# GLU gate on one core: the last load and the last two stores split by rows, in place of eight column chunks of the last tile

## The chip, the cores and the metric

The kernel runs on one core of a Trainium2 chip. The time is that of one execution on the device, in microseconds (us); lower is better. A kernel is executed several times and the median is given with the lowest and the highest. All executions were fast, at a granted clock of 1.0.

The span on a profile page is a little shorter than the time of the same execution.

## The reference

```python
# x: 8192 x 8192, float32
def reference(x):
    a, b = np.split(x, 2, axis=-1)          # two halves of 4096 columns
    return a * (1 / (1 + np.exp(-b)))       # 8192 x 4096, float32
```

Every input element is read once and every output element written once: 268.44 MB in, 134.22 MB out, and a sigmoid and a multiplication per output element.

## The kernel before

A tile is 256 rows: 128 partitions with two consecutive rows each, so a partition's load is one contiguous piece of 64 KB and its store one of 32 KB. There are 32 tiles and two buffers each for input and output. SyncE issues the loads; ScalarE computes the sigmoid and also issues the stores; VectorE multiplies.

```python
x_t = x.rearrange("(n p r) m -> n p (r m)", p=P, r=PAIR)      # PAIR = 2, P = 128
out_t = out.rearrange("(n p r) m -> n p (r m)", p=P, r=PAIR)
...
for i in range(n_tiles):                                       # 32
    x_sb = pool.tile([P, in_cols], fp32)                       # two buffers each
    o_sb = pool.tile([P, out_cols], fp32)
    nc.sync.dma_start(out=x_sb, in_=x_t[i])                    # 8 MB
    n_chunks = 4 if i >= n_tiles - 1 else 1                    # the last tile only
    for r in range(PAIR):
        ...                                                    # a_all, b_all, o_all: row r
        csz = half // n_chunks
        for c in range(n_chunks):
            ...                                                # a_part, b_part, o_part: chunk c
            nc.scalar.activation(out=b_part, in_=b_part, func=SIG)
            nc.vector.tensor_mul(out=o_part, in0=a_part, in1=b_part)
            if n_chunks > 1:
                nc.scalar.dma_start(out=out_t[i, :, ...], in_=o_part)   # 512 KB
    if n_chunks == 1:
        nc.scalar.dma_start(out=out_t[i], in_=o_sb)            # 4 MB
```

The settings that the original reads from the environment are put in at their defaults here, and the branch for single rows is left out. The compiler's scheduler is free to reorder what each engine does. I call the tiles 0 to 31.

Of the kernel before, what the change touches and what calls it, by code (L numbers as in the profile page):

```python
# [2 lines left out]

# [4 lines left out]


@with_exitstack  # L10
def kernel(
    ctx: ExitStack,
    tc: tile.TileContext,
    x: bass.AP,
    out: bass.AP,
):
    nc = tc.nc
    P = nc.NUM_PARTITIONS

    PAIR = int(os.environ.get("GLU_PAIR", "2"))  # L20
    BUFS = int(os.environ.get("GLU_BUFS", "2" if PAIR == 2 else "5"))
    STORE_ENG = os.environ.get("GLU_STORE", "scalar")
    LOAD_ENG = os.environ.get("GLU_LOAD", "sync")
    TAIL_CHUNKS = int(os.environ.get("GLU_TAIL_CHUNKS", "4"))
    TAIL_ITERS = int(os.environ.get("GLU_TAIL_ITERS", "1"))

    n_rows, n_cols = x.shape
    half = n_cols // 2
    assert out.shape == (n_rows, half)

    fp32 = mybir.dt.float32
    SIG = mybir.ActivationFunctionType.Sigmoid

    def eng(name, i):
        if name == "alt":
            name = "sync" if (i % 2 == 0) else "scalar"
        return getattr(nc, name)

    pool = ctx.enter_context(tc.tile_pool(name="io", bufs=BUFS))

    if PAIR == 1:
        x_t = x.rearrange("(n p) m -> n p m", p=P)
        out_t = out.rearrange("(n p) m -> n p m", p=P)
        n_tiles = x_t.shape[0]

        for i in range(n_tiles):
            x_sb = pool.tile([P, n_cols], fp32)
            eng(LOAD_ENG, i).dma_start(out=x_sb, in_=x_t[i])

            n_chunks = TAIL_CHUNKS if i >= n_tiles - TAIL_ITERS else 1  # L50
            csz = half // n_chunks
            for c in range(n_chunks):
                lo = c * csz
                hi = lo + csz
                a_part = x_sb[:, lo:hi]
                b_part = x_sb[:, half + lo : half + hi]
                nc.scalar.activation(out=b_part, in_=b_part, func=SIG)
                nc.vector.tensor_mul(out=a_part, in0=a_part, in1=b_part)
                eng(STORE_ENG, i + 1).dma_start(out=out_t[i, :, lo:hi], in_=a_part)
    else:  # L60
        x_t = x.rearrange("(n p r) m -> n p (r m)", p=P, r=PAIR)
        out_t = out.rearrange("(n p r) m -> n p (r m)", p=P, r=PAIR)
        n_tiles = x_t.shape[0]
        in_cols = PAIR * n_cols
        out_cols = PAIR * half

        for i in range(n_tiles):
            x_sb = pool.tile([P, in_cols], fp32)
            o_sb = pool.tile([P, out_cols], fp32)
            eng(LOAD_ENG, i).dma_start(out=x_sb, in_=x_t[i])  # L70

            n_chunks = TAIL_CHUNKS if i >= n_tiles - TAIL_ITERS else 1
            for r in range(PAIR):
                a_all = x_sb[:, r * n_cols : r * n_cols + half]
                b_all = x_sb[:, r * n_cols + half : (r + 1) * n_cols]
                o_all = o_sb[:, r * half : (r + 1) * half]
                csz = half // n_chunks
                for c in range(n_chunks):
                    lo = c * csz
                    hi = lo + csz  # L80
                    a_part = a_all[:, lo:hi]
                    b_part = b_all[:, lo:hi]
                    o_part = o_all[:, lo:hi]
                    nc.scalar.activation(out=b_part, in_=b_part, func=SIG)  # L84
                    nc.vector.tensor_mul(out=o_part, in0=a_part, in1=b_part)  # L85
                    if n_chunks > 1:
                        eng(STORE_ENG, i + 1).dma_start(  # L87
                            out=out_t[i, :, r * half + lo : r * half + hi], in_=o_part
                        )
            if n_chunks == 1:  # L90
                eng(STORE_ENG, i + 1).dma_start(out=out_t[i], in_=o_sb)


# [1 line left out]
_INS = ['x']  # L95
_OUTS = [((8192, 4096), 'float32')]


# [23 lines left out]
```

## Time and profile before

| | |
|---|---|
| time, median (lowest to highest) of the first 3 runs (2 more came with the result) | 936.99 us (936.17 to 937.19) |
| span of the profiled execution | 934.1 us |
| moved by DMA | 402.67 MB |
| VectorE busy, ScalarE busy | 30%, 25% |
| DMA packet, median duration | 64 KB: 2.418 us, 32 KB: 1.213 us, 4 KB: 0.159 us |

The packet durations are read from the single DMA records of the trace. A load has 128 packets of 64 KB, a whole-tile store 128 of 32 KB, a chunk's store 128 of 4 KB. The profile counts 16 DMA engines, and from 60 to 900 us its records have 16 packets in flight for 815 of the 840 us; spread evenly over 16, 8 of each 128 packets fall to one engine.

From the page of the kernel before: its first line, the busy time of the compute engines, and the totals of the DMA.

```profile
span 934.1 us, 410 instructions
DVE 280.9 (30%) x70; ACT 230.0 (25%) x71; POOL 0.2 (0%) x4
...
DMA packets 10226, 402.67 MB, mean 431 GB/s; under 512 B 1136, under 2 KB 1136, under 8 KB 2160
```

No compute engine is busy for a third of the time. The next view, the table of windows of the kernel before, shows where the DMA stands. Its columns are the stretch in us, its length, the busy time and count of VectorE, ScalarE and GpSimd, the granted clock, the busy share of the DMA engines and the GB/s moved. A packet is counted whole in the window in which it starts, so a short window can read above 1.

```profile
60.00:900.00 840.00, 254.06 (x58) 206.55 (x58) 0.00 (x0) 1.00 1.00 433
900.00:915.00 15.00, 0.00 (x0) 0.17 (x1) 0.00 (x0) 1.00 1.02 441
915.00:925.00 10.00, 6.99 (x6) 5.90 (x7) 0.00 (x0) 1.00 0.94 400
925.00:932.00 7.00, 2.36 (x2) 1.83 (x2) 0.00 (x0) 1.00 1.01 413
932.00:935.00 3.00, 0.00 (x0) 0.00 (x0) 0.00 (x0) 1.00 0.04 18
```

Over 840 us the share is 1.00 at 433 GB/s, and it stays near 1 until 932 us, two microseconds before the end.

The chain of work that ended last tells another story. This is its end in the kernel before (start us, us, what):

```profile
869.31 45.44 DMA x_sb<-in_x_dram
...
914.83 1.06 ACT x_sb L84
...
915.91 3.51 DVE o_sb L85 x3
...
925.92 1.23 DVE o_sb L85
927.14 1.14 DVEq L117
```

Read alone, it says that the last load, landed at 914.75 us, and the chunked computation behind it end the span, so that an earlier start of that computation would pay. It follows the compute engines; it does not show that the DMA engines, meanwhile, never stopped. The issues and landings do. First the store of tile 30, from the view of DMA issues for the window 898 to 899 us, then the page's line for the eight chunk stores (size of one, median us from issue to landing):

```profile
out_dram<-o_sb ACTq DMA_DIRECT2D x1, 4096.0 KB, 24.9
...
out_dram<-o_sb ACTq DMA_DIRECT2D x8, 512.0 KB, 6.3
```

The store of tile 30, issued at 898.35 us, lands only at 923.2. Each chunk store takes a median of 6.3 us, though moving 512 KB at 433 GB/s takes 1.2 us: they stand in a queue. The timeline of the kernel before has their issues (start, us, engine, line, what):

```profile
898.35 0.34 ACTq L91 DMA_DIRECT2D out_dram<-o_sb  x1
914.83 2.95 ACT L84 ACTIVATE x_sb<-x_sb 128x1024 f32<-128x1024 f32 x3 [21.79 <-DMA x_sb<-in_x_dram]
...
917.17 2.61 ACTq L87 DMA_DIRECT2D out_dram<-o_sb  x3
...
927.18 1.47 ACTq L87 DMA_DIRECT2D out_dram<-o_sb  x2
```

### The profile page before, as it was taken

The page shows a single profiled execution, that of the slowest core. Times are in us where ns is not written, and L with a number is a line of the kernel's source. Part 1 is how long each engine was busy: PE and PEld are TensorE (multiplying, and loading weights), DVE is VectorE, ACT ScalarE, POOL GpSimd, SP SyncE. Part 2 cuts the span into 40 slices and gives each one's busy share as a digit, 9 for nine tenths or more (in the row PEclk, how much of TensorE's full clock was granted, in tenths as well). Part 3 has the DMA queues.
Part 4 walks back from the last instruction along what each step waited for, and adds up shares of the span by engine and source line. Part 5 has one row for each costly group of instructions (what it writes and reads, how often), then busy time and mean ns, then how long its engine had stood idle before and what let it go on. Part 6 is the DMA issues. An engine that isn't in the chain of part 4 may idle for free.

```text
span 934.1 us, 410 instructions
## 1 busy us (share of the span) xinstructions
DVE 280.9 (30%) x70; ACT 230.0 (25%) x71; POOL 0.2 (0%) x4
## 2 busy tenths in 40 slices
DVE  0333321333213332133321333312333123331234
ACT  0313331133311333113332033320233202333023
POOL 0000000000000000000000000000000000000000
DMA  9999999999999999999999999999999999999998
GB/s 404 404 449 427 427 449 427 427 434 464 404 441 434 428 449 425 451 408 462 410 429 446 425 450 420 453 408 453 421 429 446 424 452 429 441 411 450 424 449 359
DMA packets 10226, 402.67 MB, mean 431 GB/s; under 512 B 1136, under 2 KB 1136, under 8 KB 2160
## 3 DMA queue, kind: packets, MB, share of 16 engines
q1 hardware_dynamic: 4608, 268.44, 66.5%
q10 hardware_dynamic: 5616, 134.22, 33.3%
q14 instruction: 2, 0.02, 0.0%
HBM read 268.44 MB, written 134.22 MB: 431 GB/s over the span
## 4 chain that ended last, share of the span: by engine, by line
DMA 78%; DVE 15%; ACT 6%; issue 0%; DVEq 0%; ACTq 0%; SPq 0%
DMA x_sb<-in_x_dram 78%; DVE o_sb L85 15%; ACT x_sb L84 6%; DVEq L117 0%; ACTq L87 0%; SPq L70 0%; ACTq L84 0%
## 5 line engine op out<-in xcount | busy, mean ns | idle before, releaser
L85 DVE TENSOR_TENSOR o_sb<-x_sb 128x4096 f32<-128x4096 f32 (+1 forms) x70 | 280.9, 4056 | 647.3 <-ACT x_sb L84 647.3
L84 ACT ACTIVATE x_sb<-x_sb 128x4096 f32<-128x4096 f32 (+1 forms) x70 | 228.7, 3315 | 696.1 <-DMA x_sb<-in_x_dram 692.0
L84 ACT ACT_TABLE_LOAD x1 | 1.3, 1283 | 0.7 <-PEq L106 0.7
L106 POOL MEMSET const-bfloat16-1.0<- 128x1 bf16 x1 | 0.1, 102 | 0.0
L106 POOL MEMSET const-uint8-127<- 128x1 uint8 x1 | 0.1, 102 | 0.0
L106 POOL MEMSET const-float32-1.0<- 128x1 f32 x1 | 0.1, 99 | 0.0
L106 POOL MEMSET const-float32-0.0<- 128x1 f32 x1 | 0.1, 98 | 0.2 <-issue 0.2
## 6 DMA issues: line engine op xcount, KB each, us to landing
out_dram<-o_sb ACTq DMA_DIRECT2D x31, 4096.0 KB, 41.8
out_dram<-o_sb ACTq DMA_DIRECT2D x8, 512.0 KB, 6.3
x_sb<-in_x_dram SPq DMA_DIRECT2D x32, 45.5
```

What stands on the lines that cost most here:

```text
L84: nc.scalar.activation(out=b_part, in_=b_part, func=SIG)
L85: nc.vector.tensor_mul(out=o_part, in0=a_part, in1=b_part)
L106: nc = _bacc.Bacc("TRN2", target_bir_lowering=False, num_devices=1)
```

## The change

Its intent is a shorter tail: the last tile can start when its first row has arrived, and the stores of tiles 30 and 31 leave row by row. ScalarE is taken away from the scheduler and works in program order. The rest of the diff removes settings and an unused branch.

```diff
+    ctx.enter_context(tc.manual_schedule(engines={mybir.EngineType.Activation}))
     for i in range(n_tiles):
+        last = i == n_tiles - 1
+        store_rows = i >= n_tiles - 2
...
-            eng(LOAD_ENG, i).dma_start(out=x_sb, in_=x_t[i])
-            n_chunks = TAIL_CHUNKS if i >= n_tiles - TAIL_ITERS else 1
+        if last:
+            for r in range(R):                                   # two loads of 4 MB
+                row = slice(r * n_cols, (r + 1) * n_cols)
+                nc.sync.dma_start(out=x_sb[:, row], in_=x_t[i, :, row])
+        else:
+            nc.sync.dma_start(out=x_sb, in_=x_t[i])
+        for r in range(R):
+            n = 2 if last else 1                                 # 2048-column pieces
...
             nc.scalar.activation(...)
             nc.vector.tensor_mul(...)
-                    if n_chunks > 1:
-                        eng(STORE_ENG, i + 1).dma_start(...)     # 512 KB
-            if n_chunks == 1:
-                eng(STORE_ENG, i + 1).dma_start(out=out_t[i], in_=o_sb)
+            if store_rows:
+                row = slice(r * half, (r + 1) * half)
+                nc.scalar.dma_start(out=out_t[i, :, row], in_=o_sb[:, row])   # 2 MB
+        if not store_rows:
+            nc.scalar.dma_start(out=out_t[i], in_=o_sb)
```

The bytes are the same. What differs is the size of the pieces: per partition, the last load comes in 32 KB pieces instead of 64 KB, and the stores of tiles 30 and 31 go in 16 KB pieces instead of 32 KB and 4 KB.

More of the change, by code (lines that the diff above doesn't have):

```diff
@@ L1 @@
-import os
 from contextlib import ExitStack
@@ L5 @@
 import concourse.tile as tile
-from concourse import bass_utils, mybir
+from concourse import mybir
 from concourse._compat import with_exitstack
@@ L18 @@
     P = nc.NUM_PARTITIONS
-    PAIR = int(os.environ.get("GLU_PAIR", "2"))
-    BUFS = int(os.environ.get("GLU_BUFS", "2" if PAIR == 2 else "5"))
-    STORE_ENG = os.environ.get("GLU_STORE", "scalar")
-    LOAD_ENG = os.environ.get("GLU_LOAD", "sync")
-    TAIL_CHUNKS = int(os.environ.get("GLU_TAIL_CHUNKS", "4"))
-    TAIL_ITERS = int(os.environ.get("GLU_TAIL_ITERS", "1"))
+    fp32 = mybir.dt.float32
+    SIG = mybir.ActivationFunctionType.Sigmoid
     n_rows, n_cols = x.shape
     half = n_cols // 2
-    assert out.shape == (n_rows, half)
@@ L31 @@
-    fp32 = mybir.dt.float32
-    SIG = mybir.ActivationFunctionType.Sigmoid
-    def eng(name, i):
-        if name == "alt":
-            name = "sync" if (i % 2 == 0) else "scalar"
-        return getattr(nc, name)
-    pool = ctx.enter_context(tc.tile_pool(name="io", bufs=BUFS))
-    if PAIR == 1:
-        x_t = x.rearrange("(n p) m -> n p m", p=P)
-        out_t = out.rearrange("(n p) m -> n p m", p=P)
-        n_tiles = x_t.shape[0]
-        for i in range(n_tiles):
-            x_sb = pool.tile([P, n_cols], fp32)
-            eng(LOAD_ENG, i).dma_start(out=x_sb, in_=x_t[i])
-            n_chunks = TAIL_CHUNKS if i >= n_tiles - TAIL_ITERS else 1
-            csz = half // n_chunks
-            for c in range(n_chunks):
-                lo = c * csz
-                hi = lo + csz
-                a_part = x_sb[:, lo:hi]
-                b_part = x_sb[:, half + lo : half + hi]
-                nc.scalar.activation(out=b_part, in_=b_part, func=SIG)
-                nc.vector.tensor_mul(out=a_part, in0=a_part, in1=b_part)
-                eng(STORE_ENG, i + 1).dma_start(out=out_t[i, :, lo:hi], in_=a_part)
-    else:
-        x_t = x.rearrange("(n p r) m -> n p (r m)", p=P, r=PAIR)
-        out_t = out.rearrange("(n p r) m -> n p (r m)", p=P, r=PAIR)
-        n_tiles = x_t.shape[0]
-        in_cols = PAIR * n_cols
-        out_cols = PAIR * half
-        for i in range(n_tiles):
-            x_sb = pool.tile([P, in_cols], fp32)
-            o_sb = pool.tile([P, out_cols], fp32)
-            eng(LOAD_ENG, i).dma_start(out=x_sb, in_=x_t[i])
-            n_chunks = TAIL_CHUNKS if i >= n_tiles - TAIL_ITERS else 1
-            for r in range(PAIR):
-                a_all = x_sb[:, r * n_cols : r * n_cols + half]
-                b_all = x_sb[:, r * n_cols + half : (r + 1) * n_cols]
-                o_all = o_sb[:, r * half : (r + 1) * half]
-                csz = half // n_chunks
-                for c in range(n_chunks):
-                    lo = c * csz
-                    hi = lo + csz
-                    a_part = a_all[:, lo:hi]
-                    b_part = b_all[:, lo:hi]
-                    o_part = o_all[:, lo:hi]
-                    nc.scalar.activation(out=b_part, in_=b_part, func=SIG)
-                    nc.vector.tensor_mul(out=o_part, in0=a_part, in1=b_part)
-                    if n_chunks > 1:
-                        eng(STORE_ENG, i + 1).dma_start(
-                            out=out_t[i, :, r * half + lo : r * half + hi], in_=o_part
-                        )
-            if n_chunks == 1:
-                eng(STORE_ENG, i + 1).dma_start(out=out_t[i], in_=o_sb)
@@ new lines @@
+    R = 2
+    n_tiles = n_rows // (P * R)
+    x_t = x.rearrange("(n p r) m -> n p (r m)", p=P, r=R)
+    out_t = out.rearrange("(n p r) m -> n p (r m)", p=P, r=R)
+    pool = ctx.enter_context(tc.tile_pool(name="io", bufs=2))
+    ctx.enter_context(tc.manual_schedule(engines={mybir.EngineType.Activation}))
+    for i in range(n_tiles):
+        last = i == n_tiles - 1
+        store_rows = i >= n_tiles - 2
+        x_sb = pool.tile([P, R * n_cols], fp32)
+        o_sb = pool.tile([P, R * half], fp32)
+        if last:
[6 more added lines that the diff above has]
+            n = 2 if last else 1
+            w = half // n
+            for c in range(n):
+                lo = r * n_cols + c * w
+                a = x_sb[:, lo : lo + w]
+                b = x_sb[:, lo + half : lo + half + w]
+                o = o_sb[:, r * half + c * w : r * half + (c + 1) * w]
+                nc.scalar.activation(out=b, in_=b, func=SIG)
+                nc.vector.tensor_mul(out=o, in0=a, in1=b)
+            if store_rows:
[3 more added lines that the diff above has]
+            nc.scalar.dma_start(out=out_t[i], in_=o_sb)
```

## The prediction

The sum stays the time before, less 0.4 us of packet overhead, plus a bubble of 0 to 1 us, and was put at 936.8 us. The sharing of 1:1 is the author's estimate from the trace of the kernel before. Its delays can be read from the same trace: the first load is issued at 0.73 us and its first packet starts at 1.73 us; the last packet ends at 932.8 us, 1.4 us before the end of the span, after an uneven finish that costs 0.7 us.

> **What bounds the kernel now.** The DMA engines, nearly everywhere. 402.67 MB move in a span of 934.1 us (page). The table of equal windows shows 434 GB/s and a DMA share of 1.00 in every 29 us stretch from 60 to 901 us, and 405 GB/s (0.95) in the last one. [...] The chain of waits ends with the last load (landed 914.75 us) and the chunked tail, but the window table shows the engines still 0.9 to 1.1 busy until about 932 us, draining stores that had queued. The store of the last but one tile, issued at 898.35, lands only at 923.2; the eight 512 KB stores, issued 917.2 to 928.3, take 4.9 to 7.6 us, queued. About 2 us of latency close the span.
>
> **What changes.** Not the bytes. The last 8 MB load becomes two of 4 MB (32 KB instead of 64 KB per partition); the last two tiles are stored as four 2 MB stores (16 KB per partition) instead of one 4 MB and eight 512 KB ones. The last tile's compute is four 2048-column pairs instead of eight of 1024. ScalarE is issued in program order.
>
> **Costs.** DMA packet durations in the trace: 64 KB 2.418 us, 32 KB 1.213, 4 KB 0.159 (64 x 0.159 = 10.2 us per engine for 4.19 MB). My estimate for a 16 KB packet is 0.61 us, so the last tile takes 9.8 us: 0.4 us saved. ScalarE/VectorE for 128x2048 between 1.05/1.22 us (1024) and 3.61/4.42 us (4096): 1.9 and 2.3 us.
>
> **Order of the tail (estimate).** [...] with 64 KB load and 32 KB store packets, a store lands 41.8 us after issue, 1.4 periods, so stores advance at half the load's rate. With 32 KB load packets against 32 KB store packets they share 1:1, so *loads get slower and stores faster*: the first half lands near 904 us, the second near 919. At 918 some 15 store packets of 16 KB are left per engine, 9.2 us, to about 927. After the second half lands: 1.9 + 2 x 2.3 us + issue puts the last 2 MB store on the queue at about 926 and its first data near 927: a bubble of 0 to 1 us. Then 4.9 us of data and 2 of latency: a span of 934 us, as before.
>
> So the last tile's earlier start is off the critical path: the DMA queue was never empty. The gain is 0.4 us of packet overhead less a possible bubble. **Predicted 936.8 us, 80% range 935.4 to 938.2; faster by over 2%: 0.01, within 2%: 0.98, slower by over 2%: 0.01.**
>
> **Right or wrong, in the profile after.** Right if the span is 933 to 935 us; the two half loads land about 15 us apart, the second 2 to 6 us later than 914.75; the last store, 2 MB, is issued near 926 and lands 6 to 8 us later; DMA stays near 1.0 until about 932; earlier tiles keep their 29.0 us period.
>
> **What would make it wrong.** The two half loads proceeding together instead of in order; the queue running dry before the last store (up to +3 us); row-split transfers off 434 GB/s; program order on ScalarE disturbing the steady state.

## The result, and the profile after

| | before | after |
|---|---|---|
| time, median (lowest to highest) | 936.99 us (936.17 to 937.19), 5 runs | 936.90 us (936.62 to 937.04), 5 runs |
| ratio, 95% interval | | 1.0001 (0.9989 to 1.0013) |
| span of the profiled execution | 934.1 us | 934.6 us |

A ratio here is the mean time of one kernel's fast runs over the mean time of the other kernel's fast runs of the same rounds, so it is not quite the ratio of the medians quoted. The two kernels take the same time.

From the page of the kernel after:

```profile
span 934.6 us, 397 instructions
DVE 280.7 (30%) x66; ACT 229.6 (25%) x67; POOL 0.2 (0%) x4
...
DMA packets 9650, 402.67 MB, mean 431 GB/s; under 512 B 1072, under 2 KB 1072, under 8 KB 1072
```

The table of windows of the kernel after, columns as before:

```profile
60.00:900.00 840.00, 251.12 (x58) 206.66 (x58) 0.00 (x0) 1.00 1.00 433
900.00:915.00 15.00, 7.53 (x3) 3.71 (x2) 0.00 (x0) 1.00 1.03 445
915.00:925.00 10.00, 3.34 (x2) 3.71 (x2) 0.00 (x0) 1.00 0.96 410
925.00:932.00 7.00, 1.16 (x1) 0.00 (x0) 0.00 (x0) 1.00 0.96 410
932.00:935.00 3.00, 0.00 (x0) 0.00 (x0) 0.00 (x0) 1.00 0.03 11
```

VectorE's 7.53 us of work between 900 and 915 us, where before it had none, are the early start that the change wanted. The DMA columns hardly differ, and the experiments below show that they decide the end.

The timeline of the kernel after:

```profile
894.58 0.34 ACTq L62 DMA_DIRECT2D out_dram<-o_sb  x1
...
903.07 0.34 ACTq L62 DMA_DIRECT2D out_dram<-o_sb  x1
905.22 3.71 ACT L58 ACTIVATE x_sb<-x_sb 128x2048 f32<-128x2048 f32 x2 [6.63 <-DMA x_sb<-in_x_dram]
...
911.68 0.34 ACTq L62 DMA_DIRECT2D out_dram<-o_sb  x1
919.72 3.71 ACT L58 ACTIVATE x_sb<-x_sb 128x2048 f32<-128x2048 f32 x2 [10.79 <-DMA x_sb<-in_x_dram]
...
926.19 0.34 ACTq L62 DMA_DIRECT2D out_dram<-o_sb  x1
```

The last store's time from issue to landing, from the view of DMA issues of the kernel after for the window 925 to 940 us:

```profile
out_dram<-o_sb ACTq DMA_DIRECT2D x1, 2048.0 KB, 7.5
```

The first row's data is used from 905.22 us, 9.6 us earlier than anything of the last tile before. The second row's is used from 919.72 us, 4.9 us later than before. The last store is issued at 926.19 us and lands 7.5 us later, at 933.7. Of the start of 9.6 us, nothing reaches the end. The earlier tiles keep their period: from 60 us on, up to the activations of tile 30, those of one tile begin 28.9 to 29.3 us after those of the tile before, in both kernels.

### The profile page after: what moved, and what is told of

Read it like the earlier page. It is cut to its first block, busy times and chain, and to the rows that moved or that the text cites. A ratio compares the mean times of both kernels' runs of the same rounds, so it can differ in the third digit from the quotient of the medians.

```text
span 934.6 us, 397 instructions
## 1 busy us (share of the span) xinstructions
DVE 280.7 (30%) x66; ACT 229.6 (25%) x67; POOL 0.2 (0%) x4
## 4 chain that ended last, share of the span: by engine, by line
DMA 78%; DVE 14%; ACT 6%; DVEq 0%; issue 0%; SPq 0%; ACTq 0%
DMA x_sb<-in_x_dram 78%; DVE o_sb L59 14%; ACT x_sb L58 6%; DVEq L90 0%; SPq L48 0%; SPq L46 0%; ACTq L58 0%
```

## The experiments

Two theories stand against each other. The **queue theory**: the 16 DMA engines have work without a break from 1.7 us to the end, so only bytes, rate and idle engine time count; a tail is good enough as soon as it issues each store before the queue runs dry, and anything better is worth nothing. The **compute-chain theory**, which the chain of waits suggests: what is computed after the last load ends the span, so the change must have gained something there and lost it elsewhere (in slower loads, smaller packets or the fixed order on ScalarE).

Eight kernels ran, in two groups with five rounds each. Each group shared nine runs of the kernel before on its chip: a median of 936.33 us (936.12 to 937.04) in the group of the first four, and 937.05 us (936.34 to 937.68) in that of the last four. All gave the right result, except the last one, which is wrong on purpose.

### 1. More work in the first row, and in the second

```diff
                 nc.vector.tensor_mul(out=o, in0=a, in1=b)
+                if last and r == 0:          # extra_row1: r == 1
+                    nc.vector.tensor_mul(out=o, in0=a, in1=b)
```

> The kernel after, with each VectorE multiply of the last tile's first row done twice (about +4.5 us of VectorE work before the third-last... i.e. before the first 2 MB store of the last tile; the result stays right). Queue theory (the DMA queue decides, and the first row's store only has to be issued before the queue would run dry, at about 922 us): that store moves from 911.7 to about 916.2 us, the span stays within 0.5 us of the kernel after, ratio to before 1.000. Compute-chain theory (what the last tile computes after its load lands is what ends the span): +4 us or so, ratio 1.004 to 1.005.

> The same extra work, but in the last tile's second row. Queue theory: the last store is issued at about 930.7 instead of 926.2 us, the queue runs dry at about 927.3, so the engines idle some 4.4 us and the time grows by about 4.4 us (ratio 1.0047). Compute-chain theory: the same growth as for the first row. If both kernels are as fast as after, neither theory holds and something else ends the span.

Measured: with the extra work in the first row 936.54 us (936.33 to 937.03), ratio to before 1.0002 (0.9989 to 1.0014); in the second row 940.04 us (939.06 to 940.62), ratio 1.0036 (1.0023 to 1.0049).

The timeline of the run with extra work in the first row shows that the work was really there:

```profile
906.07 3.71 ACT L58 ACTIVATE x_sb<-x_sb 128x2048 f32<-128x2048 f32 x2 [6.04 <-DMA x_sb<-in_x_dram]
...
916.94 0.34 ACTq L64 DMA_DIRECT2D out_dram<-o_sb  x1
```

The store follows 10.9 us after the activation's start, against 6.5 us in the kernel after (905.22 to 911.68), and it costs nothing that the times show. (In this execution the last store went out 0.8 us later than in the kernel after, at 927.00 against 926.19 us, and 0.8 us of engine time was idle before it. That is not the extra work: this execution was late before it, with the last tile's loads issued from 871.37 against 870.00 us.) The same 4.4 us in the second row cost about 3.3 us (mean of the runs against the mean of before). The windows of that run show how they become time:

```profile
919.00:926.00 7.00, 5.12 (x3) 3.65 (x2) 0.00 (x0) 1.00 1.01 433
926.00:928.00 2.00, 2.00 (x2) 0.00 (x0) 0.00 (x0) 1.00 0.39 164
928.00:930.00 2.00, 1.78 (x1) 0.00 (x0) 0.00 (x0) 1.00 0.00 0
930.00:936.00 6.00, 0.00 (x0) 0.00 (x0) 0.00 (x0) 1.00 0.83 350
```

VectorE works while the DMA engines stand still. The timeline has the last store:

```profile
929.82 0.34 ACTq L64 DMA_DIRECT2D out_dram<-o_sb  x1
```

Its first packet starts at 930.66 us, with nothing queued before it. So work of the last tile costs time only once it makes the DMA queue run dry. The compute-chain theory expected both to cost the same, and falls.

### 2. Tile 30 stored whole again

```diff
-        store_rows = i >= n_tiles - 2
+        store_rows = last
```

> The kernel after, with the last tile but one stored by one 4 MB DMA (32 KB per partition) again. Packet-sharing theory (each engine alternates one load packet with one store packet): the second half load now meets 32 KB instead of 16 KB store packets, falls from two thirds to half of the engines, and lands at 924 to 925 instead of 919.7 us; the last store is issued at about 931 and the queue is dry for 4 to 5 us before it; time +4 to +5 us (ratio about 1.005). Byte-sharing or no-effect theory (the split of this store only lets it start earlier, and the queue was full anyway): second half lands at about 920, time within 0.5 us of after.

Measured: 939.87 us (939.27 to 940.84), ratio 1.0037 (1.0023 to 1.0051). By the means this is 3.5 us more than before: without the split of this one store, the rest of the change is a loss. Its gain is not that it lets the store leave earlier. From the timeline of this run:

```profile
900.17 0.34 ACTq L64 DMA_DIRECT2D out_dram<-o_sb  x1
...
924.59 3.71 ACT L58 ACTIVATE x_sb<-x_sb 128x2048 f32<-128x2048 f32 x2 [15.01 <-DMA x_sb<-in_x_dram]
...
931.06 0.34 ACTq L62 DMA_DIRECT2D out_dram<-o_sb  x1
```

Stored whole it is issued at 900.17 us, while the store of tile 29 is still to land at 902.9. What changes is how fast the *load* runs. These are the shares of the two queues between 906 and 918 us, when the second half load is on its way (q1 carries the loads, q10 the stores); first the kernel after, then this run:

```profile
q1 hardware_dynamic: 112, 3.31, 63.9%
q10 hardware_dynamic: 123, 1.75, 34.1%
```

```profile
q10 hardware_dynamic: 80, 2.62, 50.6%
q1 hardware_dynamic: 80, 2.62, 50.5%
```

The columns after the queue's name are packets, MB and the share of the engines' time. In both, the two queues advance by nearly equal numbers of packets (27 of the records counted in the kernel after are of 4 bytes; without them it is 101 against 107). Joined end to start, since the records do not name their engine, the packets of this run in that window follow each other as load, store, load, store in all of 160 steps. So the load had 63.9% of the engines with packets twice as large as the store's, and 50.5% with equal ones. The second half load is used from 924.59 us instead of 919.72. The first half load shows the same: between 886 and 901 us the loads had 68.5% of the engines before (64 KB against 32 KB) and 50.5% after (32 KB against 32 KB). The late load then makes the last store late, at 931.06 us, with an idle queue before it.

### 3. Only the split of the stores, and only the split of the load

```diff
# load_whole: the kernel after
-        if last:
+        if False:                      # one load of 8 MB for every tile
# load_split_only: the kernel before
+            if i == n_tiles - 1:
+                for r in range(PAIR):
+                    row = slice(r * n_cols, (r + 1) * n_cols)
+                    nc.sync.dma_start(out=x_sb[:, row], in_=x_t[i, :, row])
+            else:
```

> The kernel after with the last load in one 8 MB DMA again, stores by rows kept. Queue theory: the load lands at about 914.5 us, the first row's store is issued at about 921.5, just as the queue runs dry (about 922.5), the second row's at about 928.4, with its first data at 929.6 against a queue dry at 927.5 to 928: idle 1.5 to 2 us, time +1.5 to +2.5 us (ratio about 1.002). If the split of the load were worth its whole head start, the loss would be 7 us or more (ratio 1.008).

> The kernel before with only the last load split in two halves; stores as before (4 MB for the last tile but one, eight of 512 KB for the last). Queue and packet-sharing theory: both halves share 1:1 with 32 KB store packets, land at about 905 and 924 us; the chunked second row then issues its last store at about 931 us while the queue is dry from about 928: time +0.5 to +2.5 us (ratio 1.0005 to 1.0025). Theory that an earlier first half is a gain by itself: faster than before by several us (ratio 0.995 or less).

Measured: with the load whole and the stores by rows 936.98 us (936.67 to 937.39), ratio 1.0006 (0.9993 to 1.0018); with only the load split 937.01 us (936.34 to 937.40), ratio 0.9999 (0.9987 to 1.0012). Both are below their expected ranges, and neither differs clearly from before. The times of the single steps came as expected: the whole load is used from 914.90 us and its last store issued at 928.22; the split loads are used from 906.07 and 924.35 us, the second late because it met 32 KB store packets (the load had 48.0% of the engines from 906 to 915 us, against 63.9% in the kernel after from 906 to 918). The idle engine time came too (1.9 and 1.5 us between 915 and 931.5 us, from the packet records), but it turned into less time than I had counted. The accounting below gives a likely reason. The rivals' sizes, 7 us or more lost or several us gained, are excluded.

### 4. No tail at all

```diff
-    TAIL_CHUNKS = int(os.environ.get("GLU_TAIL_CHUNKS", "4"))
+    TAIL_CHUNKS = int(os.environ.get("GLU_TAIL_CHUNKS", "1"))
```

> The kernel before with the last tile not chunked at all: one load, two activations and multiplies, one 4 MB store. Queue theory: the store is issued at about 927.4 us (914.8 + 12.4), its first data comes at about 928.6, the queue (the store of the last tile but one) is dry from about 922; idle 6 to 7 us, time +6 to +7 us (ratio 1.0065 to 1.0075). This says what either tail is worth against none. No-effect theory: ratio 1.000.

Measured: 942.04 us (941.41 to 942.15), ratio 1.0052 (1.0038 to 1.0065). The windows of this run:

```profile
915.00:922.00 7.00, 2.65 (x1) 6.30 (x2) 0.00 (x0) 1.00 0.92 398
922.00:924.00 2.00, 2.00 (x2) 0.82 (x1) 0.00 (x0) 1.00 0.04 16
924.00:929.00 5.00, 4.11 (x1) 0.00 (x0) 0.00 (x0) 1.00 0.08 33
929.00:939.00 10.00, 0.00 (x0) 0.00 (x0) 0.00 (x0) 1.00 0.94 403
```

The engines are idle for 6.7 us in all, and all of them at once from 923.7 us to the first packet of the last store at 928.98. So some tail is worth about 5 us, and the tail of before already had all of it.

### 5. ScalarE left to the scheduler

```diff
-    ctx.enter_context(tc.manual_schedule(engines={mybir.EngineType.Activation}))
```

> The kernel after without the fixed program order on ScalarE; the compiler then puts the first activation of the last tile's second row ahead of the first row's store, so that this store can only be issued after the second half load has landed and been activated (about 921.7 instead of 911.7 us). Queue theory: the queue is dry only at about 922.5 us, so ten us later costs 0 to 1 us (ratio 1.000 to 1.001). Theory that the program order is a real part of the change: +4 us or more (ratio 1.004 or more).

Measured: 936.83 us (936.24 to 937.26), ratio 0.9998 (0.9985 to 1.0010). The timeline of this run:

```profile
920.19 1.91 ACT L58 ACTIVATE x_sb<-x_sb 128x2048 f32<-128x2048 f32 x1 [10.79 <-DMA x_sb<-in_x_dram]
920.20 0.34 ACTq L62 DMA_DIRECT2D out_dram<-o_sb  x1
```

The first row's store, ready near 912 us, stood behind an activation that waited for the second half load, and left at 920.20 us: 1.5 us earlier than expected, because it did not wait for that activation's end. That is 8.5 us later than in the kernel after, and free: the queue had work until then. The fixed program order is no measurable part of the result.

### 6. The data movement alone

```diff
+        o_sb = pool.tile([P, out_cols], fp32)
+        nc.vector.memset(o_sb, 0.0)
         for i in range(n_tiles):
             x_sb = pool.tile([P, in_cols], fp32)
-            o_sb = pool.tile([P, out_cols], fp32)
...
-            for r in range(PAIR):
+            for r in range(0):         # nothing is computed; zeros are stored
```

> Wrong result on purpose: the same 32 loads of 8 MB, and 32 stores of 4 MB of zeros that wait for nothing but one memset; no ScalarE work, no VectorE multiply. It measures what the data movement alone takes. Queue theory: 16 engines busy for 930 to 932 us, so the time is 934 to 936.5 us, at most 3 us (0.3%) below before; no arrangement of the tail could gain more. Theory that the tail's waits cost real time in both kernels: 5 us or more below before (ratio 0.995 or less).

Measured: 935.95 us (935.67 to 937.01), ratio 0.9992 (0.9980 to 1.0005). From its page:

```profile
span 933.9 us, 129 instructions
DVE 6.9 (1%) x1; POOL 0.2 (0%) x4
```

The same loads and stores, freed of all dependencies on computation, take 0.7 us less than before by the means, and even that is within the interval. This run has another order, however: its stores run ahead and the last of them ends at 710 us, so that only loads are left at the end. From 715 to 925 us they alone keep the DMA share at 1.00, at 433 GB/s, the rate of the mixture in the kernel before. So the run does not show the best tail; it shows that these bytes at this rate fill the time in this order too, and that waiting for computation cost before little or nothing. Of what a better end could still win, its 0.5 us of idle engine time (next section) gives the size. With these transfers there is nothing left that would beat both kernels clearly.

### The accounting

From the packet records I summed, over the time from 900 us to the end of the last packet, the unused part of the 16 engines (one idle engine out of 16 for 1 us counts 1/16 us). The column after it says how much of it falls in the last 2.5 us before the last packet's end. All numbers belong to the profiled execution of each kernel; the last column is worked out before rounding.

| kernel | span, us | idle, us | of it at the very end | span less idle |
|---|---|---|---|---|
| before | 934.1 | 0.7 | 0.7 | 933.5 |
| after | 934.6 | 1.3 | 1.2 | 933.3 |
| extra_row0 | 934.8 | 1.5 | 0.6 | 933.3 |
| extra_row1 | 937.1 | 3.7 | 0.1 | 933.4 |
| t30_whole | 938.2 | 4.7 | 0.1 | 933.5 |
| load_whole | 935.3 | 2.0 | 0.1 | 933.3 |
| load_split_only | 935.3 | 1.6 | 0.1 | 933.6 |
| no_chunks | 940.0 | 6.8 | 0.1 | 933.3 |
| sched | 935.0 | 1.4 | 1.2 | 933.6 |
| dma_floor | 933.9 | 0.5 | 0.5 | 933.4 |

The last column is constant within 0.4 us while the spans differ by 6 us. The bytes are the same in all ten, and the engines' rate while they work is nearly so; what is left to differ is idle engine time, and it accounts for the spans of these ten executions to within 0.4 us.

It also suggests why the losses in experiment 3 came out small. Where the engines never all stood idle at once, they were out of step and finished their last packets at different times, which left 0.5 to 1.2 us unused at the end. Where it ran dry, all 16 started again together (in load_whole their first packets after the gap start between 929.06 and 929.21 us), ended together and left only 0.1 us. So a gap gives back about 0.6 us against the end of before, and 1.1 us against that of after. That is not the whole of it: the two kernels of experiment 3 span 1.2 us more than before in the table, but take only 0.5 us more and 0.1 us less by the means of all runs. Their profiled executions were the slowest of five, while the span of 934.1 us of before fits only the fastest of its five runs. What the slower, untraced executions of before did at their end is not known, so this reason is not shown to be the only one.

## Why the prediction was right

**The bound.** Right. The DMA is full from 1.7 us, the first packet, to 932 us (a mean share of 1.00 by the packet records of the kernel before); the movement alone takes 935.95 us.

**The change removes and adds no bytes, and the head start is off the critical path.** Right. Experiments 1 and 5 show it directly: 4.4 us more work, or a store 8.5 us later, cost nothing.

**Loads get slower and stores faster when their packets become equal.** Right. I put the two half loads at 904 and 919 us and 15 us apart; they are used from 905.22 and 919.72, 14.5 us apart. Experiment 2 shows the effect by itself: with the store beside it in 32 KB packets, the second half load is used from 924.59 us. The evidence given in the prediction was weaker than the claim: a store that lands 1.4 periods after its issue does not show that the two queues advance by equal numbers of packets, and stores carry half of the loads' bytes in any case. The packet counts show it (68 load and 64 store packets from 886 to 901 us in the kernel before).

**The last store, issued near 926 us, lands 6 to 8 us later.** Right: 926.19 us, and 7.5 us. Of the bubble of 0 to 1 us, 0.1 us is found in the records between 915 and 931.5 us.

**The gain of 0.4 us from larger packets.** This term was mis-sized. I took it from the durations of single packets (0.159 us for 4 KB; the 0.61 us that I put for 16 KB is what they take, 0.611). But records of 4 KB packets overlap: in the middle of that phase the shares of the engines add up to 1.03. Moved bytes say it better: 420 GB/s with 4 KB packets (923.5 to 930.5 us in the kernel before) against 431 GB/s with 16 KB (919.5 to 925.5 us in the kernel after). For 4.19 MB that is 9.99 against 9.72 us, a gain of under 0.3 us.

**The fixed 2 us at the end.** Roughly right as a sum, but not equal in both: the time from the last packet to the end of the span is 1.4 us in the kernel before and 1.3 us in the kernel after, and the uneven finish ahead of the last packet costs 0.7 us in the former and 1.2 us in the latter (profiled executions). That 0.5 us is enough to cancel the packets' gain. But it is one execution against one, and differences this small are below the scatter of the runs, about 1 us from lowest to highest. That the predicted 936.8 us lies within 0.1 us of the measured median is therefore luck; that the time stays the same is not.

**The delay from an issue to its first packet,** which I had put at 1 us or a little more (1.00 us for the first load of the kernel before), is 0.84 us on an empty queue in four runs (extra_row1, t30_whole, load_whole, no_chunks). This and the even finish after a gap both make the losses smaller than I expected; in experiments 1 to 4 they were too large by about 0.5 to 2 us.

## What to carry to other kernels

In a kernel that keeps its DMA engines full, judge a tail by one question: is each store issued before the queue runs dry, by at least the delay to its first packet (0.84 us here)? Up to that point an earlier start was worth nothing here (9.6 us earlier for the last tile, at a ratio of 1.0001), and a chain of waits that ends in computation does not contradict this; measure the movement alone before tuning further. Where a load and a store shared the engines here, the load's share went with the packet sizes (68.5% with 64 KB against 32 KB, 63.9% with 32 KB against 16 KB, 50.5% with 32 KB against 32 KB), so splitting one transfer changed the speed of the other. Splitting the last load while the store beside it stays whole made the second half late in two runs (used from 924.59 and 924.35 us). It cost 3.5 us where the last row then left in one store of 2 MB (t30_whole), and nothing measurable where it left in four of 512 KB (load_split_only), whose first pieces, issued from 926.69 us, filled part of the gap.
